# Output projection of a hybrid attention encoder: 256-column matmuls made 512 columns wide

## Chip, cores and metric

The kernel runs on one core of a Trainium2 chip. The metric is the device time of one execution in microseconds (us), as a median over runs.

## What is computed

Two layers act on x, 512 tokens by 1024 features. A layer normalises x, projects it to queries, keys, values and gates of two head groups (A: 8 heads of neighbourhood attention on an 8 by 64 grid; B: 4 heads of differential attention), multiplies each group's output by SiLU of its gate, and sends the concatenation y (512 by 1024; features 0 to 511 are group A, 512 to 1023 group B) through one output projection that is added to x. A last RMS norm closes the trunk.

```python
    h = rmsnorm(x, norm_g[l])
    proj = h @ w_in[l]
    ...
    y = jnp.concatenate([out_a * jax.nn.silu(g_a), out_b * jax.nn.silu(g_b)], axis=-1)
    x = x + y @ w_out[l]
return rmsnorm(x, final_g)
```

All is float32. The kernel keeps the precision by splitting each operand of a projection into a high part of type fp32r and a low part (the difference); a product is three matmuls: high times high, high times low, low times high.

## The kernel before

Tokens stand in four tiles of 128 (t = 0 to 3), features in eight chunks of 128 (kc). A weight unit is 1024 rows by 256 columns. `load_raw` (L79) reads one half of its rows (4 chunks, 512 KB) from DRAM on SP's queue into the tile `wraw` (two buffers). `load_unit` (L89) makes the high part `wh` by a ScalarE cast (L99) and the low part `wl` by a subtraction (L101), on GpSimd, or on VectorE for the first half of the units 16 to 19 of each 20, which are the output projection's; `wh` and `wl` have two buffers each. `Weights` hands the units out in the order of `seq` (L404 on): each `get` is followed by a `prefetch`, which emits the load and the conversion of the next unit.

Projections come in two forms. `proj_fm` (L245, matmul at L252) has the weights stationary and streams 512 tokens: 24 matmuls of 512 columns. `proj_tm` (L257, matmul at L267) has 128 tokens stationary and streams 256 weight columns: 24 matmuls of 256 columns (8 chunks times 3 terms) into half of a PSUM bank.

PSUM has eight banks: three in the pool `ps_p` (projections, tile `pp`), one in `ps_v` (attention output, `pv`), two each in `ps_s` (scores) and `ps_t` (transposes).

The output stage stands at the end of a layer. The gated outputs y are split into `yTh` and `yTl` (L569 on). Then four column units (`un`), and in each four token tiles: `proj_tm` over the chunks in the order 4, 5, 6, 7, 0, 1, 2, 3 (group B's features are ready first); VectorE adds the residual from PSUM (L592), ScalarE squares with a row sum into `sst` (L593), VectorE multiplies by the norm's weight (L595). In the last unit the row sums are added (L598), `rstd` makes the factor on GpSimd (L210, L212), and the normalised row is scaled. In layer 0 that is `norm_apply` (L226): two scalings on VectorE, eight transposes on TensorE (L234), and the split into `hTh` and `hTl` on ScalarE (L205) and VectorE (L206), which the next layer's projections read. In the last layer ScalarE (L601) and VectorE (L602) scale 384 and 640 columns, and the result is written to DRAM (L604).

The order of the instructions on each engine is not the order of the program text: a planner that simulates a timeline (`schedule_with_timeline_sim`) chooses it ahead of time, and on the chip each engine then keeps its order. So matmuls of the last attention heads stand among the first of the output stage, and the transposes and the next value projection among its last.

Of the kernel before, what the change touches and what calls it, by code (L numbers as in the profile page):

```python
# [9 lines left out]
F32 = mybir.dt.float32  # L10
F32R = mybir.dt.float32r
AF = mybir.ActivationFunctionType
ALU = mybir.AluOpType
# [3 lines left out]
P = 128  # L17
S = 512
D = 1024
# [4 lines left out]
NB = 4  # L24
# [20 lines left out]
def hybrid_encoder(ctx: ExitStack, tc: tile.TileContext, x, norm_g, w_in, na_rpb,  # L45
                   lambda_q1, lambda_k1, lambda_q2, lambda_k2,
                   subln_g, t5_table, w_out, final_g, na_mask, t5_onehot, out):
    nc = tc.nc
# [8 lines left out]
    small = ctx.enter_context(tc.tile_pool(name="small", bufs=6))  # L57
    dram = ctx.enter_context(tc.tile_pool(name="dram", bufs=1, space=DRAM))
    ps_p = ctx.enter_context(tc.tile_pool(name="ps_p", bufs=3, space=PSUM))
# [15 lines left out]

    # ---------------------------------------------------------------- weights
    unit_no = [0]

    def load_raw(parts, hf):  # L79
        r = wp.tile([P, 4, 256], F32, name="wraw", bufs=WRAW_BUFS)  # L80
        c = 0
        for src in parts:
            n_c = src.shape[1]
            nc.sync.dma_start(out=r[:, :, c:c + n_c],
                              in_=src.rearrange("(k p) c -> p k c", p=P)[:, 4 * hf:4 * hf + 4, :])
            c += n_c
        return r
# [35 lines left out]

    # ------------------------------------------------------- position biases
    tb_d = dram.tile([4, 1024], F32, name="tb_d")
# [58 lines left out]

    # ------------------------------------------------------------- lambdas
    def lambdas(l):
# [20 lines left out]

    # ---------------------------------------------------------------- norm
    def rstd(ss):
        G.tensor_scalar(out=ss, in0=ss, scalar1=1.0 / D, scalar2=1e-6, op0=ALU.mult, op1=ALU.add)  # L210
        rs = small.tile([P, 1], F32, name="rs")
        G.tensor_tensor(out=rs, in0=ss, in1=nhalf[:, 0:1], op=ALU.pow)  # L212
        return rs
# [29 lines left out]

    # --------------------------------------------------------- projections
    def proj_fm(w, col, c0=64):  # L245
# [55 lines left out]

    # ---------------------------------------------------------- attention B
    def attn_b(h, q, k, vt, yb, nlam, sg, yout):
# [57 lines left out]

    # ---------------------------------------------------------- attention A
    def attn_a(l, hd, half, q, k, vt, s_out):
# [37 lines left out]

    # ------------------------------------------------------------- schedule
    o_b = 2048
    seq = []  # L404
    for l in range(DEPTH):
        wi, wo = w_in[l], w_out[l]
        def qkc(o, i):
            return ((o + i * P, P), (o + 512 + i * P, P))

        def vgc(c):  # L410
            return ((c, 256),)

        unit = {"VB": lambda i: vgc(o_b + 1024 + 256 * i), "VA": lambda i: vgc(1024 + 256 * i),
                "QB": lambda i: qkc(o_b, i), "QA": lambda i: qkc(0, i),
                "GB": lambda i: vgc(o_b + 1536 + 256 * i), "GA": lambda i: vgc(1536 + 256 * i)}
        cols = [unit[u[:2]](int(u[2])) for u in ORDER if u[:2] in unit]
        seq += [[wi[:, c:c + n] for c, n in u] for u in cols]
        seq += [[wo[:, c:c + 256]] for c in (0, 256, 512, 768)]
    W = Weights(seq)
# [89 lines left out]
    for l in range(DEPTH):  # L509
# [73 lines left out]
        xn = [x2[:, i, :] for x2 in [big.tile([P, 2, D], F32, name="xn", tag="v") for _ in range(2)] for i in range(2)]  # L583
        sst = small.tile([P, NB, 4], F32, name="sst", bufs=1)
        yh, yl = ([y[:, i, :] for y in yt for i in range(2)] for yt in (yTh, yTl))
        for un in range(4):
            w = W.get()
            W.prefetch()
            for t in range(NB):
                pp = proj_tm(w, t * P, yh, yl, (4, 5, 6, 7, 0, 1, 2, 3))  # L590
                cs = slice(un * 256, (un + 1) * 256)
                V.tensor_tensor(out=xt[t][:, cs], in0=pp[:, 0:256], in1=xt[t][:, cs], op=ALU.add)  # L592
                A.activation(out=xn[t][:, cs], in_=xt[t][:, cs], func=AF.Square,  # L593
                             accum_out=sst[:, t, un:un + 1])
                V.tensor_tensor(out=xn[t][:, cs], in0=xt[t][:, cs], in1=g_bc[:, cs], op=ALU.mult)  # L595
                if un == 3:
                    ss = small.tile([P, 1], F32, name="ss")
                    V.tensor_reduce(out=ss, in_=sst[:, t, :], axis=mybir.AxisListType.X, op=ALU.add)  # L598
                    rs = rstd(ss)
                    if last:  # L600
                        A.activation(out=xn[t][:, 0:384], in_=xn[t][:, 0:384], func=AF.Copy, scale=rs)  # L601
                        V.tensor_scalar_mul(xn[t][:, 384:D], xn[t][:, 384:D], rs)  # L602
                        for i in range(2):
                            nc.sync.dma_start(out=out_v[2 * t + i], in_=xn[t][64 * i:64 * i + 64])  # L604
                    else:
                        nc.sync.dma_start(out=xs_d[t], in_=xt[t])
                        norm_apply(t, xt[t], None, xn[t], rs)

# [53 lines left out]
```

## Time and profile before

| | us |
|---|---|
| median of 3 runs | 633.57 |
| lowest, highest run | 631.53, 634.60 |
| span of the profiled execution | 630.6 |
| TensorE matmuls busy | 591.7 |
| VectorE busy | 422.3 |
| ScalarE busy | 324.6 |
| GpSimd busy | 277.3 |

The profile is one execution, with the time from its first to its last instruction as span. Engines are called PE (TensorE matmuls), PEld (its weight loads), DVE (VectorE), ACT (ScalarE), POOL (GpSimd) and SP. A line such as L267 is a line of the kernel. An instruction is written as engine, line, operation, output<-input tiles, size. In square brackets stands how long the engine was idle before it and what ended that. Matmuls overlap one another: the printed time of one is from its start to its modelled end, longer than the distance to the next.

### The profile page before, as it was taken

Reading aid. Unit: us, or ns where it says so; the run is one execution under the profiler, and the core shown is the slowest. Engines: PE = TensorE matmul, PEld = TensorE weight load, DVE = VectorE, ACT = ScalarE, POOL = GpSimd, SP = SyncE. Lnnn points to the kernel's source line nnn. Section 1 sums busy time; section 2 is a strip of 40 time slices with the busy share of each in tenths; the row PEclk is TensorE's granted clock in tenths of the full one; section 3 lists DMA queues with packets and bytes.
Section 4 is the critical chain, followed back from the end, with each engine's and each line's share of the span. In section 5 each row is a group of like instructions: output and inputs, shape, how many; then the busy total and the mean of one; then the engine's idle time right before and its main releaser. Section 6 shows DMA issues by size and latency. Waiting matters only on the chain.

```text
span 630.6 us, 10037 instructions
## 1 busy us (share of the span) xinstructions
PE 591.7 (94%) x3626; PEld 522.3 (83%) x3626; DVE 422.3 (67%) x907; ACT 324.6 (51%) x706; POOL 277.3 (44%) x232
## 2 busy tenths in 40 slices
PE   4799699999899999999999999999989999999992
PEld 3678597888799878889999898888879878889992
DVE  3552354997988868874564257798888968874542
ACT  3343353864766555744343455666567646654421
POOL 2341422444456747743143633344535665733111
PEclk9799899999999999999999999999999999999997
DMA  6566746552442454264454452342343444355204
GB/s 145 129 124 192 213 147 197 134 136 78 109 119 55 143 129 133 85 171 146 134 168 135 123 144 86 90 114 63 88 107 93 116 116 116 101 167 168 68 1 134
DMA packets 77448, 77.57 MB, mean 123 GB/s; under 512 B 9906, under 2 KB 71346, under 8 KB 76374
## 3 DMA queue, kind: packets, MB, share of 16 engines
q1 hardware_dynamic: 75926, 74.53, 41.7%
q0 software_dynamic: 1472, 2.40, 2.3%
q8 instruction: 29, 0.48, 0.3%
q14 instruction: 21, 0.17, 0.1%
HBM read 63.16 MB, written 9.37 MB: 115 GB/s over the span
## 4 chain that ended last, share of the span: by engine, by line
PE 58%; DMA 14%; DVE 10%; issue 5%; POOL 5%; SPq 5%; ACT 3%; POOLq 0%; ACTq 0%; DVEq 0%
PE pp L252 25%; PE pp L267 22%; DMA wraw<-in_w_in_dram 4%; DMA y<-in_x_dram 4%; SPq L135 3%; DVE ea L382 2%; POOL wl L101 2%; DMA yb_d<-tb_d 2%; POOL ba L179 2%; PE pv L338 2%; DVE kt L291 2%; DVE w4k L329 1%; PE pt L333 1%; PE st L316 1%; DMA rs_d<-rsb 1%
## 5 line engine op out<-in xcount | busy, mean ns | idle before, releaser
L101 POOL TENSOR_TENSOR wl<-wraw,wh 128x1024 fp32r<-128x1024 f32 x68 | 166.2, 2462 | 192.5 <-ACT wh L99 124.9
L99 ACT CAST wh<-wraw 128x1024 fp32r<-128x1024 f32 x78 | 78.8, 1046 | 72.2 <-DMA wraw<-in_w_in_dram 28.9
L252 PE MATMUL pp<-hTh,wh 128*128 128x512 f32 x384 | 103.4, 397 | 3.2 <-DVE kt L291 3.2
L252 PE MATMUL pp<-hTh,wl 128*128 128x512 f32 x384 | 106.3, 398 | 0.0
L252 PE MATMUL pp<-hTl,wh 128*128 128x512 f32 x384 | 104.5, 398 | 0.0
L252 PEld LDWEIGHTS pp<-hTh,wh 128*128 128x128 f32 x384 | 70.4, 188 | 17.7 <-issue 3.6
L252 PEld LDWEIGHTS pp<-hTh,wl 128*128 128x128 f32 x384 | 70.3, 189 | 14.5 <-issue 0.5
L252 PEld LDWEIGHTS pp<-hTl,wh 128*128 128x128 f32 x384 | 70.2, 188 | 13.9
L267 PE MATMUL pp<-wh,hTh 128*128 128x256 f32 x256 | 72.3, 302 | 7.7 <-ACT hTh L205 4.5
L267 PE MATMUL pp<-wh,yTh 128*128 128x256 f32 x256 | 72.4, 283 | 0.0
L267 PE MATMUL pp<-wl,yTh 128*128 128x256 f32 x256 | 72.3, 283 | 0.0
L267 PE MATMUL pp<-wh,yTl 128*128 128x256 f32 x256 | 71.9, 283 | 0.0
L267 PE MATMUL pp<-wh,hTl 128*128 128x256 f32 x256 | 70.3, 293 | 0.0
L206 DVE TENSOR_TENSOR ptl<-pt,pth 128x256 fp32r<-128x256 f32 (+1 forms) x96 | 48.2, 507 | 31.6 <-ACT pth L205 30.7
L267 PE MATMUL pp<-wl,hTh 128*128 128x256 f32 x256 | 68.9, 287 | 0.0
L205 ACT CAST pth<-pt 128x256 fp32r<-128x256 f32 (+1 forms) x96 | 42.0, 443 | 43.1 <-PE pt L333 29.3
L382 DVE TENSOR_SCALAR ea<-ea,rza 128x256 f32<-128x256 f32 x64 | 58.5, 914 | 1.8
L267 PEld LDWEIGHTS pp<-wh,hTh 128*128 128x128 f32 x256 | 49.3, 202 | 10.9 <-ACT hTh L205 5.0
L179 POOL TENSOR_TENSOR ba<-nmask,ya 128x256 f32<-128x256 f32 (+1 forms) x64 | 39.6, 650 | 32.3 <-DVE mna L376 18.5
L319 DVE CUSTOM_DVE_ANT_0 lt<-st,yb 128x512 f32<-128x512 f32 x64 | 43.5, 685 | 11.2 <-PE st L317 10.7
L267 PEld LDWEIGHTS pp<-wh,hTl 128*128 128x128 f32 x256 | 48.8, 199 | 0.8
L267 PEld LDWEIGHTS pp<-wh,yTh 128*128 128x128 f32 x256 | 49.1, 192 | 0.2
(111 smaller groups left out, 1141.0 us busy)
## 6 DMA issues: line engine op xcount, KB each, us to landing
wraw<-in_w_in_dram SPq DMA_DIRECT2D x32, 512.0 KB
wraw<-in_w_in_dram SPq DMA_DIRECT2D x64, 256.0 KB
kt<-kt SPq DMA_DIRECT2D x16, 512.0 KB
wraw<-in_w_out_dram SPq DMA_DIRECT2D x16, 512.0 KB
y<-in_x_dram SPq DMA_DIRECT2D x16, 256.0 KB
ya_d<-rp_d SPq DMA_DIRECT2D x32, 120.0 KB
ya<-ya_d SPq DMA_DIRECT2D x16, 240.0 KB
yb<-yb_d SPq DMA_DIRECT2D x8, 280.0 KB
```

Of the source, the lines that this page charges most:

```text
L99: A.copy(out=wh[:, ks, :], in_=r)
L101: eng.tensor_tensor(out=wl[:, ks, :], in0=r, in1=wh[:, ks, :].bitcast(F32), op=ALU.subtract)
L135: eng.dma_start(out=dst[:, i * C8:(i + 1) * C8, :], in_=bass.AP(tensor=src.tensor, offset=src.offset + base - step * r - C8 * b, ap=[[pitc ...
L179: G.tensor_tensor(out=ba[:, i0:i0 + n], in0=_view(nmask, i0 * C8, [[C8, n], [0, ROWS], [1, C8]]), in1=_view(y, w0, [[C8, n], [RPW, ROWS], ...
L205: A.copy(out=oh, in_=ps)
L206: V.tensor_tensor(out=ol, in0=ps, in1=oh.bitcast(F32), op=ALU.subtract)
L252: T.matmul(out=pp, lhsT=a[:, kc, cs], rhs=b[:, kc, c0:c0 + S], start=(n == 0), stop=(n == 3 * KC - 1))
L267: T.matmul(out=pp[:, 0:256], lhsT=a[kc][:, c0:c0 + P], rhs=b[:, kc, :], start=(n == 0), stop=(n == 3 * KC - 1))
L291: V.tensor_tensor(out=kl, in0=src, in1=kh.bitcast(F32), op=ALU.subtract)
L319: V.tensor_tensor_reduce(out=lt, in0=st, in1=yb[:, 48 - 16 * qt:560 - 16 * qt], scale=1.0, scalar=3e38, op0=ALU.add, op1=ALU.min, accum_ou ...
L338: T.matmul(out=pv[:, qp * 256:(qp + 1) * 256], lhsT=vt[:, kt, h % 2, vs, :], rhs=pp[:, kt, :], start=(n == 0), stop=(n == 11))
L382: V.tensor_scalar_mul(e, e, rz)
```

## The change

The output projection's weights are taken in pieces of 512 rows by 512 columns, in place of units of 1024 rows by 256 columns: for each column half first the rows of group B, then those of group A. A piece has as many bytes as a unit and lies in the same tiles, seen through `half_k` as four chunks of 512 columns; its two raw loads are one DMA each, of two chunks. For each of the two column halves, four PSUM banks (three `pp` and the one `pv`) hold the four token tiles while both pieces pass: 12 matmuls of 512 columns for each tile and piece. After the second piece a tile is evacuated with 512-column operations, and `sst` has two columns for each tile.

```diff
+    def half_k(z):
+        return z.rearrange("p (k a) c -> p k (a c)", a=2)
     def load_raw(parts, hf):
         r = wp.tile([P, 4, 256], F32, name="wraw", bufs=WRAW_BUFS)
+        if parts[0].shape[1] == S:
+            nc.sync.dma_start(out=half_k(r), in_=parts[0].rearrange("(k p) c -> p k c", p=P)[:, 2 * hf:2 * hf + 2, :])
+            return r
...
-        seq += [[wo[:, c:c + 256]] for c in (0, 256, 512, 768)]
+        seq += [[wo[r:r + S, c:c + S]] for c in (0, S) for r in (S, 0)]
...
-        for un in range(4):
-            w = W.get()
-            W.prefetch()
-            for t in range(NB):
-                pp = proj_tm(w, t * P, yh, yl, (4, 5, 6, 7, 0, 1, 2, 3))
-                cs = slice(un * 256, (un + 1) * 256)
-                V.tensor_tensor(out=xt[t][:, cs], in0=pp[:, 0:256], in1=xt[t][:, cs], op=ALU.add)
...
-                if un == 3:
...
+        def out_tile(un, t, cs, pp):
+            V.tensor_tensor(out=xt[t][:, cs], in0=pp, in1=xt[t][:, cs], op=ALU.add)
+            A.activation(out=xn[t][:, cs], in_=xt[t][:, cs], func=AF.Square,
+                         accum_out=sst[:, t, un:un + 1])
+            V.tensor_tensor(out=xn[t][:, cs], in0=xt[t][:, cs], in1=g_bc[:, cs], op=ALU.mult)
+            if un == 1:
...
+        for un in range(2):
+            pps = [ps_p.tile([P, S], F32, name="pp") for _ in range(3)] + [ps_v.tile([P, S], F32, name="pv")]
+            cs = slice(un * S, (un + 1) * S)
+            for half, c0 in enumerate((4, 0)):
+                wh, wl = (half_k(z) for z in W.get())
+                W.prefetch()
+                for t in range(NB):
+                    for kc in range(4):
+                        for i, (a, b) in enumerate(((yh, wh), (yh, wl), (yl, wh))):
+                            T.matmul(out=pps[t], lhsT=a[c0 + kc][:, t * P:(t + 1) * P], rhs=b[:, kc, :],
+                                     start=(half + kc + i == 0), stop=(half == 1 and kc == 3 and i == 2))
+                    if half == 1:
+                        out_tile(un, t, cs, pps[t])
```

What `out_tile` does for `un == 1` is what the loop did for `un == 3`.

## Rows read from the trace of the kernel before

**Rows 1.** The page: busy time of the engines; the chain that ended last, by engine.

```profile
PE 591.7 (94%) x3626; PEld 522.3 (83%) x3626; DVE 422.3 (67%) x907; ACT 324.6 (51%) x706; POOL 277.3 (44%) x232
...
PE 58%; DMA 14%; DVE 10%; issue 5%; POOL 5%; SPq 5%; ACT 3%; POOLq 0%; ACTq 0%; DVEq 0%
```

**Rows 2.** The chain in order of time, layer 1's stage: start us, us, what.

```profile
572.66 0.48 PE pp L267 x4
...
573.98 45.49 PE pp L267 x379
```

**Rows 3.** The same chain, end of layer 0's attention and its output stage.

```profile
270.23 7.43 PE pp L252 x32
...
278.12 3.97 PE pp L252 x17
...
283.40 44.42 PE pp L267 x369
```

**Rows 4.** Busy time by stretch, instructions in brackets, granted clock: ten us of layer 1's stage.

```profile
590.00:600.00 10.00, 10.00 (x86) 10.00 (x85) 4.88 (x9) 3.94 (x10) 1.37 (x1) 1.00 0.18 61
```

**Rows 5.** Timeline of ACT, POOL and DVE around a weight conversion: start us, us, instruction.

```profile
584.94 1.99 ACT L99 CAST wh<-wraw 128x1024 fp32r<-128x1024 f32 x2 [1.91 <-PE pp L267]
...
587.07 2.44 POOL L101 TENSOR_TENSOR wl<-wraw,wh 128x1024 fp32r<-128x1024 f32 x1 [8.94 <-ACT wh L99]
...
587.38 2.41 DVE L595 TENSOR_TENSOR xn<-y,g_bc 128x256 f32<-128x256 f32 x1
```

**Rows 6.** Timeline of VectorE: last read of the attention's bank in layer 1.

```profile
575.53 0.69 DVE L399 SCALAR_TENSOR_TENSOR y<-pv,tmpa 64x512 f32<-64x512 f32 x1
```

**Rows 7.** Tiles yTh, yTl, hTl: 512-column operations, ns min/median/max, first and last start.

```profile
L205 ACT CAST yTh<-y x16: 608/619/624, 265.3 to 578.2; 128x512 fp32r<-128x512 f32 x16
...
L206 DVE TENSOR_TENSOR yTl<-y,yTh x16: 679/692/2893, 266.2 to 578.8; 128x512 fp32r<-128x512 f32 x16
...
L206 DVE TENSOR_TENSOR hTl<-pt,hTh x16: 675/692/692, 15.6 to 341.7; 128x512 fp32r<-128x512 f32 x16
```

**Rows 8.** Timeline of VectorE, then ScalarE: last column unit of layer 1.

```profile
610.86 0.42 DVE L592 TENSOR_TENSOR y<-pp,y 128x256 f32<-128x256 f32 x1 [1.45 <-PE pp L267]
...
613.32 0.55 DVE L602 TENSOR_SCALAR xn<-xn,rs 128x640 f32<-128x640 f32 x1 [0.97 <-POOL rs L212]
...
613.79 0.42 DVE L592 TENSOR_TENSOR y<-pp,y 128x256 f32<-128x256 f32 x1
...
619.50 0.42 DVE L592 TENSOR_TENSOR y<-pp,y 128x256 f32<-128x256 f32 x1 [1.30 <-PE pp L267]
...
619.84 0.55 DVE L602 TENSOR_SCALAR xn<-xn,rs 128x640 f32<-128x640 f32 x1
...
620.50 0.42 DVE L595 TENSOR_TENSOR xn<-y,g_bc 128x256 f32<-128x256 f32 x1
...
621.93 0.55 DVE L602 TENSOR_SCALAR xn<-xn,rs 128x640 f32<-128x640 f32 x1 [0.94 <-POOL rs L212]
...
619.14 0.61 ACT L601 ACTIVATE xn<-xn,rs 128x384 f32<-128x384 f32 x1 [1.47 <-POOL rs L212]
...
619.95 0.42 ACT L593 ACTIVATE xn<-y 128x256 f32<-128x256 f32 x1 [0.20 <-DVE y L592]
```

**Rows 9.** Timeline of DVE, POOL, ACT and PE at the layer boundary.

```profile
331.26 0.42 DVE L592 TENSOR_TENSOR y<-pp,y 128x256 f32<-128x256 f32 x1
...
333.70 0.14 DVE L598 TENSOR_REDUCE ss<-sst 128x1 f32<-128x4 f32 x1
...
331.10 4.93 POOL L101 TENSOR_TENSOR wl<-wraw,wh 128x1024 fp32r<-128x1024 f32 x2 [1.27 <-ACT wh L99]
...
336.12 0.19 POOL L210 TENSOR_SCALAR ss<-ss 128x1 f32<-128x1 f32 x1
...
339.48 0.59 ACT L205 CAST hTh<-pt 128x512 fp32r<-128x512 f32 x1 [1.72 <-PE pt L234]
...
341.15 1.09 PE L252 MATMUL pp<-hTh,wh 128*128 128x512 f32 x4
```

More of the change, by code (lines that the diff above doesn't have):

```diff
@@ L583, in hybrid_encoder @@
         xn = [x2[:, i, :] for x2 in [big.tile([P, 2, D], F32, name="xn", tag="v") for _ in range(2)] for i in range(2)]
-        sst = small.tile([P, NB, 4], F32, name="sst", bufs=1)
+        sst = small.tile([P, NB, 2], F32, name="sst", bufs=1)
         yh, yl = ([y[:, i, :] for y in yt for i in range(2)] for yt in (yTh, yTl))
-        for un in range(4):
-            w = W.get()
-            W.prefetch()
-            for t in range(NB):
-                pp = proj_tm(w, t * P, yh, yl, (4, 5, 6, 7, 0, 1, 2, 3))
-                cs = slice(un * 256, (un + 1) * 256)
-                V.tensor_tensor(out=xt[t][:, cs], in0=pp[:, 0:256], in1=xt[t][:, cs], op=ALU.add)
-                A.activation(out=xn[t][:, cs], in_=xt[t][:, cs], func=AF.Square,
-                             accum_out=sst[:, t, un:un + 1])
-                V.tensor_tensor(out=xn[t][:, cs], in0=xt[t][:, cs], in1=g_bc[:, cs], op=ALU.mult)
-                if un == 3:
[L597 to L607, printed above, removed]
@@ new lines, in out_tile @@
+        def out_tile(un, t, cs, pp):
[4 more added lines that the diff above has]
+            if un == 1:
+                ss = small.tile([P, 1], F32, name="ss")
+                V.tensor_reduce(out=ss, in_=sst[:, t, :], axis=mybir.AxisListType.X, op=ALU.add)
+                rs = rstd(ss)
+                if last:
+                    A.activation(out=xn[t][:, 0:384], in_=xn[t][:, 0:384], func=AF.Copy, scale=rs)
+                    V.tensor_scalar_mul(xn[t][:, 384:D], xn[t][:, 384:D], rs)
+                    for i in range(2):
+                        nc.sync.dma_start(out=out_v[2 * t + i], in_=xn[t][64 * i:64 * i + 64])
+                else:
+                    nc.sync.dma_start(out=xs_d[t], in_=xt[t])
+                    norm_apply(t, xt[t], None, xn[t], rs)
```

## Prediction

> **What bounds the kernel.** I read the page first. TensorE is busy 94% of the span and has 58% of the chain that ended last; VectorE, the next engine, is busy 67% [rows 1]. The reader should note that the profiled execution spans 630.6 us while the median of the three timed runs is 633.57 us: some 3 us lie around the span, and I add every difference to the median. The chain in order of time then says what the stage under change waits for: in layer 1 it is one unbroken piece of 379 matmuls of line 267, 45.49 us, from 573.98 us to 619.47 us, and only then a tail of vector work [rows 2]; in layer 0 it is the same, 369 matmuls in 44.42 us [rows 3], and it begins and ends on TensorE there too. The table of stretches agrees: in 10 us of the stage TensorE and its weight loads are busy 10.00 us each at full clock, VectorE 4.88 us [rows 4]. So in this stage a nanosecond saved per matmul comes off the end, and work of the other engines costs nothing until TensorE waits for it. It could at two places: after the last matmul of layer 1, where nothing is left to hide it, and at the boundary.
>
> **TensorE's part.** The stage has 2 layers x 4 column units x 4 token tiles x 24 = 768 matmuls of 256 columns; after the change 2 x 2 x 2 x 4 x 12 = 384 of 512 columns. Products and columns streamed are the same; only what a matmul costs beyond its columns can go. The pitch, not the printed duration, is the price, as matmuls overlap: 45.49 us / 379 = 120.0 ns for 256 columns [rows 2]. For 512 columns the trace has the feature-major projections of line 252, same type, same 128x128 weight load: 32 in 7.43 us, 232.2 ns each, and 17 in 3.97 us, 233.5 ns [rows 3]. Before: 768 x 120.0 = 92.2 us. After: 384 x 232.2 = 89.2 us. The gain is 3.0 us. The other ends: by 233.5 ns it is 2.5 us. At the granted full clock (2.4 GHz) the columns alone take 106.7 and 213.3 ns, so the surplus is 13.3 ns at 256 and 18.9 ns at 512; were it a constant 13.3 ns per matmul, the pitch would be 226.6 ns and the gain 5.1 us. I take 3.0 us because thirty-two matmuls in a row are its row; 2.5 and 5.1 are kept for the range.
>
> The Trainium skill, "TensorE: Matmul & The Clock Gate", section "Wait — 56ns, not 53.3ns?", speaks for the constant: it gives a warm matmul its columns plus a fixed 2.5 ns or so whatever their number. By its own figures the gain would be an estimated 384 x 2.5 = 1.0 us; by its form with this trace's surplus at 256 columns it would be the 5.1 us. That form is the first rival. The trace agrees with neither so far, since its surplus grows with the columns, but its 512-column rows have another operand in the moving place.
>
> **Weights.** Each of the 16 raw loads of the output weights stays 512 KB, two per piece, on SP's queue at the same place; they only carry 512-column rows. The casts and subtractions keep their number, size and engine. A piece lasts 48 x 0.232 = 11.1 us instead of a unit's 96 x 0.120 = 11.5 us. In layer 1 a unit's weights are cast from 584.94 us, as soon as the buffer is free, and the last subtraction ends at 589.51 us, while they are needed a unit later, at about 596.4 us [rows 5]. That cover of 7 us becomes 6.5. I cost all of this at nothing; without the cover it would be up to 4.6 us a piece.
>
> **Banks.** Three projection banks and the attention's one are now held for two pieces (22.3 us), where a bank was held for one tile. The last reader before that, of the attention's bank, is the last neighbourhood head, which ends at 576.22 us [rows 6]; the last gate is read ahead of it. The first tile may start at 572.66 us [rows 2]; the third, which needs the last gate's bank, then starts 5.6 us later (578.2), the fourth, in the attention's bank, 8.4 us later (581.0). Covers: 2.0 us or more, and 4.8 us. For the second column half a bank's matmuls end three tiles (8.4 us) before it is needed, and its addition has that long. The next projection of layer 1 takes banks in the same turn as before, and the attention's bank is wanted only by the first attention head. Cost: nothing. That group A's features are wanted 11 us later is worth nothing either: TensorE has no stall there to win.
>
> **Evacuation and the tail.** There are 8 evacuations of 512 columns per layer in place of 16 of 256. VectorE's and ScalarE's total falls a little, which is worth nothing as both are half idle here. But what follows the last matmul gets longer: addition, square and multiplication each on 512 columns. VectorE takes 0.42 us on 256 columns for the addition and the multiplication [rows 8], and 0.69 us on 512, both from PSUM and from SBUF; ScalarE 0.42 us [rows 8] against 0.62 us [rows 7]. So +0.27 +0.20 +0.27 = +0.74 us on the tail that now runs from 619.50 us over the norm's factor to 621.93 us [rows 8]. One more delay can come: ScalarE's scaling of the third tile (619.14 us, 0.61 us) left ScalarE free 0.2 us before the last square [rows 8]. It comes 0.74 us later in its tile's chain, the last addition ends 0.27 us later in its own, and tiles follow each other after 12 x 0.232 = 2.79 us in place of 24 x 0.120 = 2.88: the last square is held up by some 0.3 us. The tail costs 0.74 to 1.05 us; I take 0.9, its middle. Below 0.74 it can hardly be, since the three steps follow one another. The transfers of the result (same number and size) follow as before.
>
> **The boundary.** The normalised tiles of layer 0 are transposed for layer 1 on TensorE. The last tile's chain in the trace: the addition starts at 331.26 us, behind other vector work, the reduction is done at 333.84, but GpSimd does its part at 336.12 only, since it subtracts weights from 331.10 to 336.03 [rows 9]. The longer steps (0.74 us) and some more lateness of the addition use up the 2.3 us for which the reduction's result lay there; GpSimd's subtraction is released by the end of the same matmuls as before. What is late next: the projections over all tokens start at 341.15 us with the first half of that tile's features, ready at 340.07 [rows 9], a cover of 1.1 us. I take nothing here; the other end stands under the second rival.
>
> **Sum.** -3.0 + 0.9 = -2.1 us: the span goes from 630.6 to 628.5, the median from 633.57 to 631.5 us, 0.33% less. A measurement of this kernel can tell about 0.5% (3.2 us) from no change, so this counts as the same. With the tail's ends and the pitch at 232.2 or 233.5 ns it is 631.3 to 632.1; the pitch's other end is the first rival.
>
> **Rivals.** First, the constant surplus: a matmul of 512 columns with the weights moving takes 226.6 ns. For it: the surplus has no reason in these rows to depend on the columns. Against it: every long run of line 252. Gain 5.1 - 0.9 = 4.2 us, 629.4 us, faster.
>
> Second, the vector chain, which ends slower. VectorE works in its own order, and in layer 1 the first tile's last scaling stood ahead of the second's addition [rows 8]: it came 2.46 us after its own addition (610.86 to 613.32), and the next addition 0.47 us after that (613.79). With 0.74 us more, a tile's turn is 2.46 + 0.74 + 0.47 = 3.67 us, against 2.79 us on TensorE, so the fourth tile is 3 x 0.88 = 2.6 us late. At the boundary the same 2.6 + 0.74 us stands against 1.1 us of cover: 2.2 us. Together -3.0 + 0.74 + 2.6 + 2.2 = +2.5 us, 636.1 us. If besides one 512-wide multiplication is caught by GpSimd's weight subtraction, as one of 256 columns was (2.41 us in place of 0.42) [rows 5], 1.7 us more, 637.8 us. It decides where the additions of the next tile stand behind the scaling; against it speaks that the last addition, ready first, did stand ahead of the scaling (619.50 before 619.84) [rows 8], and an order by readiness would now put every addition ahead.
>
> Third, no gain per matmul: with weights as the moving operand 512 columns take twice the 120.0 ns. Then only the tail remains: 634.5 us, the same. Against it: in the 256-column rows the moving weights show nothing special. Fourth, the order elsewhere: it is made by a simulated timeline, and the layer after the change may be ordered differently, two us either way (629.5 or 633.5 with the rest as forecast). Against it: the stage's long pieces begin 290.58 us apart in the two layers and hold 369 and 379 matmuls, so the order repeats [rows 2, 3].
>
> **Chances.** Forecast 0.58, constant surplus 0.13, vector chain 0.17, no gain 0.06, order elsewhere 0.06. Faster by over 0.5% (under 630.4): the constant surplus, half of the order, and 0.03 of the forecast, as the runs themselves scatter (631.53 to 634.60), 0.19. Slower by over 0.5% (over 636.7): two thirds of the vector chain, that with the caught multiplication or with more of it, 0.11. The rest, 0.70, is within 0.5%. The range reaches from 629.0, just under the constant surplus, to 636.2, the vector chain without the caught multiplication.
>
> **What would show it.** Line 252's pitch on the new matmuls: 384 of them, four pieces of about 11.1 us a layer, TensorE busy 10.00 of 10 us in both stages; a pitch near 226 ns speaks for the first rival, 240 for the third. The tail from the last addition to the last scaling: 2.43 us before, about 3.2 to 3.5 after. At the boundary no TensorE wait; a wait of TensorE for the split of a transposed tile, or a last addition of layer 1 more than 1 us behind the last matmul, speaks for the second rival. Wrong throughout would be: a wait of TensorE for a bank or for weights between pieces.

## The result, and the profile after

| | before | after |
|---|---|---|
| median | 633.57 us | 637.18 us |
| lowest, highest run | 630.08, 636.05 | 633.23, 641.73 |
| runs | 13 | 13 |
| span of the profiled execution | 630.6 us | 640.0 us |

The ratio is 1.0070, 95% interval 1.0046 to 1.0094: slower by 2.9 to 6.0 us, where 2.1 us less was forecast. The two spans differ by more, 9.3 us, since the profiled execution of after is its slowest (641.73 us) and 3.65 us of its span were lost ahead of the first matmul of the changed stage, in work that is the same in both kernels. So what follows compares distances inside the spans: from the first matmul of layer 0's output stage to that of layer 1's (the period), the stage itself, and the tail behind the last matmul's start.

The chain that ended last, in order of time (start us, us, what), first from layer 0's stage to the next layer's projections, then the start of layer 1's stage:

```profile
287.60 7.28 PE pp L619 x32
...
308.25 8.16 PE pp L619 x36
...
323.37 2.29 DVE xn L596
...
331.11 0.56 POOL rs L218
331.69 5.04 DVE xn L232 x2
336.74 0.61 DVE hTl L212
...
337.39 1.11 PE pt L240 x4
338.50 2.56 PE pp L273 x12
...
584.99 7.28 PE pp L619 x32
```

The new matmuls (L619) follow each other after 8.16 us / 36 = 226.7 ns, and 7.28 us / 32 = 227.5 ns. Both stages last 44.05 us from the first to the last start, against 46.68 us in layer 1 before: 2.63 us less, and 5.3 us for two layers. TensorE is busy 10.00 us in both stretches of 10 us below, and has no wait in either stage. The gain is there, then, and larger than forecast.

It is given back between the layers: there the chain runs over VectorE, with 5.04 us in two scalings (L232), before TensorE can go on at 337.39. The period, which the long pieces give as 573.98 - 283.40 = 290.58 us before [rows 2, 3], is 584.99 - 287.60 = 297.39 us after: 6.8 us longer, though it holds one shortened stage. The boundary costs 6.8 + 2.6 = 9.4 us more than before.

Busy time by stretch, with the granted clock as the eighth number (after the five engines' times): layer 0's stage, layer 1's stage, and the boundary of after:

```profile
290.00:300.00 10.00, 10.00 (x46) 8.29 (x45) 2.07 (x3) 2.63 (x3) 2.22 (x3) 1.00 0.62 202
595.00:605.00 10.00, 10.00 (x45) 8.28 (x45) 5.69 (x7) 4.18 (x8) 2.43 (x1) 1.00 0.36 105
...
330.00:334.00 4.00, 1.40 (x11) 0.95 (x9) 3.65 (x5) 3.57 (x6) 3.08 (x4) 0.89 0.65 266
334.00:338.00 4.00, 0.61 (x3) 0.61 (x4) 4.00 (x6) 0.00 (x0) 2.45 (x1) 0.50 0.48 141
338.00:342.00 4.00, 4.00 (x21) 4.00 (x20) 1.29 (x2) 0.63 (x2) 0.74 (x2) 0.50 0.40 121
```

TensorE has 0.61 us of work in the four us from 334; the granted clock is at its lower level (0.50, that is 1.2 of 2.4 GHz) in all of 334 to 342, also after the work is back: 21 instructions in 338 to 342, where the kernel with the change in layer 1 only (e1 below) has 37 at full clock:

```profile
338.00:342.00 4.00, 4.00 (x37) 4.00 (x35) 2.43 (x5) 1.32 (x3) 0.00 (x0) 1.00 0.44 131
```

The waits of TensorE from 318 to 350 us (total, times, longest), and the timelines of TensorE, VectorE, ScalarE and GpSimd that explain them:

```profile
PE pt L240 <- DVE hTl L212: 4.3, 1, 4.3
PE pp L273 <- ACT hTh L211: 1.7, 1, 1.7
```

```profile
329.86 1.03 PE L240 MATMUL pt<-ident,xn 128*128 128x128 f32 x8
332.63 0.39 PE L273 MATMUL pp<-wh,hTh 128*128 128x256 f32 x1 [1.74 <-ACT hTh L211]
...
326.70 0.88 DVE L232 TENSOR_SCALAR xn<-xn,rs 128x512 f32<-128x512 f32 x2 [0.37 <-POOL rs L218]
...
331.69 5.04 DVE L232 TENSOR_SCALAR xn<-xn,rs 128x512 f32<-128x512 f32 x2 [0.35 <-POOL rs L218]
336.66 0.68 DVE L212 TENSOR_TENSOR hTl<-pt,hTh 128x512 fp32r<-128x512 f32 x1
...
330.10 1.99 ACT L105 CAST wh<-wraw 128x1024 fp32r<-128x1024 f32 x2 [0.50 <-issue]
332.00 0.58 ACT L211 CAST hTh<-pt 128x512 fp32r<-128x512 f32 x1
...
331.11 0.55 POOL L218 TENSOR_TENSOR rs<-ss,nhalf 128x1 f32<-128x1 f32 x1
331.62 4.83 POOL L107 TENSOR_TENSOR wl<-wraw,wh 128x1024 fp32r<-128x1024 f32 x2
```

Three things come together. (a) The first tile's eight transposes (L240) now stand behind the stage's last matmul (329.62); before they stood ten matmuls ahead of its end (L234 below). So nothing of TensorE's own is left to cover what follows. (b) The cast of the transposed half (L211, 332.00) stands on ScalarE behind two weight casts (330.10): 1.7 us. (c) The third tile's two scalings on VectorE (L232) take 5.04 us in place of 0.88, for as long as GpSimd's two weight subtractions run (331.62 to 336.45); the split of the first tile's second half (L212) is queued behind them: 4.3 us. With 1.7 + 4.3 = 6.0 us of waiting and about 6 us of work at half clock (337.4 to 343.4, an estimated 3 us lost) the 9.4 us are explained but for 0.4.

Before, the weight subtraction stood in nearly the same place (331.10, 4.93 us [rows 9]), but no scaling fell into it. From the timelines of TensorE, GpSimd and VectorE before:

```profile
327.66 1.03 PE L234 MATMUL pt<-ident,xn 128*128 128x128 f32 x8
...
329.61 0.28 PE L267 MATMUL pp<-wh,yTl 128*128 128x256 f32 x1
...
329.29 0.55 POOL L212 TENSOR_TENSOR rs<-ss,nhalf 128x1 f32<-128x1 f32 x1
...
329.87 0.88 DVE L226 TENSOR_SCALAR xn<-xn,rs 128x512 f32<-128x512 f32 x2 [0.26 <-POOL rs L212]
...
336.97 0.49 DVE L226 TENSOR_SCALAR xn<-xn,rs 128x512 f32<-128x512 f32 x1 [1.33 <-POOL rs L212]
```

GpSimd's order is the same in both kernels: the third tile's factor, the two subtractions, the last tile's factor. What differs is the time of the third tile's factor. Before, it was done at 329.84 and the subtractions then still waited, 1.27 us in all, for ScalarE's cast [rows 9]; in that gap the scalings (329.87) ran undisturbed, and the last tile's (336.97) came behind the subtractions. In after the factor is done at 331.66, the cast is there, and the subtractions start at once; the scalings, which that same factor releases, start 0.07 us behind them. The factor is 1.8 us later at the same end of the stage (329.61 and 329.62). The three longer steps are 0.74 us of that. Another part comes from the first tile, whose multiplication (L596, 323.37 in the chain above) was itself caught by the unit before's subtractions, 2.29 us in place of 0.69; VectorE's later additions come behind it.

The end, VectorE and ScalarE's last tile; compare [rows 8]:

```profile
627.44 0.69 DVE L593 TENSOR_TENSOR y<-pv,y 128x512 f32<-128x512 f32 x1
628.42 0.55 DVE L603 TENSOR_SCALAR xn<-xn,rs 128x640 f32<-128x640 f32 x1 [0.29 <-POOL rs L218]
628.92 0.69 DVE L596 TENSOR_TENSOR xn<-y,g_bc 128x512 f32<-128x512 f32 x1
...
628.17 0.63 ACT L594 ACTIVATE xn<-y 128x512 f32<-128x512 f32 x1 [1.48 <-DVE y L593]
...
630.62 0.62 ACT L602 ACTIVATE xn<-xn,rs 128x384 f32<-128x384 f32 x1 [1.23 <-POOL rs L218]
```

From the last addition to the end of the last scaling it is 3.80 us, before 3.05 (619.50 to 622.55): +0.75. The whole tail, from the start of the last matmul to the end, is 12.94 us against 11.44: +1.5. How much of that is the change's is taken up below.

### The profile page after: what moved, and what is told of

It is laid out like the page before. It is cut to its first block, busy times and chain, and to the rows that moved or that the text cites. A ratio compares the mean times of both kernels' runs of the same rounds, so it can differ in the third digit from the quotient of the medians.

```text
span 640.0 us, 9199 instructions
## 1 busy us (share of the span) xinstructions
PE 593.1 (93%) x3242; PEld 507.9 (79%) x3242; DVE 416.6 (65%) x875; ACT 320.3 (50%) x674; POOL 276.3 (43%) x232
## 4 chain that ended last, share of the span: by engine, by line
PE 60%; DMA 13%; DVE 11%; issue 5%; POOL 4%; SPq 4%; ACT 2%; POOLq 0%; ACTq 0%; DVEq 0%
PE pp L258 26%; PE pp L273 11%; PE pp L619 9%; DMA y<-in_x_dram 4%; DMA wraw<-in_w_in_dram 3%; SPq L141 3%; PE pv L344 3%; DVE ea L388 3%; PE pv L619 3%; DMA yb_d<-tb_d 2%; PE st L322 2%; PE pt L339 2%; PE st L323 2%; POOL wl L107 2%; PE st L376 1%
## 5 line engine op out<-in xcount | busy, mean ns | idle before, releaser
L273 PE MATMUL pp<-wh,hTl 128*128 128x256 f32 x256 | 71.7, 299 | 0.0
L212 DVE TENSOR_TENSOR ptl<-pt,pth 128x256 fp32r<-128x256 f32 (+1 forms) x96 | 48.2, 507 | 35.0 <-ACT pth L211 34.2
L273 PE MATMUL pp<-wl,hTh 128*128 128x256 f32 x256 | 70.5, 294 | 0.0
L211 ACT CAST pth<-pt 128x256 fp32r<-128x256 f32 (+1 forms) x96 | 42.0, 442 | 45.1 <-PE pt L339 31.2
L273 PEld LDWEIGHTS pp<-wl,hTh 128*128 128x128 f32 x256 | 49.3, 201 | 0.7
L328 ACT ACTIVATE w4k<-lt,mn 128x512 f32<-128x512 f32 x64 | 46.0, 722 | 4.3 <-DVE mn L325 3.9
L385 ACT ACTIVATE ea<-ea,mna 128x256 f32<-128x256 f32 x64 | 32.8, 512 | 23.0 <-DVE mna L382 23.0
L297 DVE TENSOR_TENSOR kt<-pp,kt 64x512 fp32r<-64x512 f32 x32 | 21.9, 685 | 27.7 <-ACT kt L296 27.3
```

What stands on the lines that cost most here:

```text
L211: A.copy(out=oh, in_=ps)
L212: V.tensor_tensor(out=ol, in0=ps, in1=oh.bitcast(F32), op=ALU.subtract)
L273: T.matmul(out=pp[:, 0:256], lhsT=a[kc][:, c0:c0 + P], rhs=b[:, kc, :], start=(n == 0), stop=(n == 3 * KC - 1))
L328: A.activation(out=e[:, m, :].rearrange("p (b r c) -> p b r c", r=ROWS, c=C8), in_=lt.rearrange("p (r b c) -> p b r c", r=ROWS, c=C8), fun ...
L385: A.activation(out=e, in_=e, func=AF.Exp, bias=mn, scale=-1.0, accum_out=z[:, j:j + 1])
```

## Experiments

Each ratio is against runs of the kernel before on the same chip. Period, waits, clock (the lowest of the stretches of 4 us from 326 to 350) and tail are from each kernel's one profile; line numbers shift by a few where lines were added. A difference of the medians and one by the ratio can lie up to 1.0 us apart (after: 3.6 and 4.4 us), so the text says which is meant.

| | period us | waits of TensorE at the boundary us | lowest clock | tail us | median us (before) | ratio, 95% interval |
|---|---|---|---|---|---|---|
| before | 290.6 | none | 1.00 | 11.44 | 633.57 | |
| after | 297.4 | 4.3 + 1.7 | 0.50 | 12.94 | 637.18 (633.57) | 1.0070 (1.0046 to 1.0094) |
| e1 | 292.3 | none | 1.00 | 12.76 | 633.23 (636.0) | 0.9966 (0.9942 to 0.9991) |
| e2 | 297.6 | 4.3 + 1.7 | 0.51 | 12.21 | 640.42 (636.0) | 1.0079 (1.0052 to 1.0106) |
| e3 | 293.6 | 2.3 + 0.2 | 0.62 | 12.70 | 634.38 (636.0) | 0.9983 (0.9962 to 1.0003) |
| e4 | 294.8 | 2.4 + 1.7 | 0.50 | 12.91 | 637.06 (636.0) | 1.0032 (1.0005 to 1.0058) |
| e5 | 296.4 | 5.0 + 0.2 | 0.50 | 12.89 | 638.65 (635.45) | 1.0051 (1.0027 to 1.0075) |
| e6 | 290.1 | 0.7 | 1.00 | 12.92 | 632.67 (635.45) | 0.9950 (0.9926 to 0.9975) |
| e7 | 292.3 | 2.3 | 0.74 | 12.18 | 635.11 (635.45) | 0.9998 (0.9977 to 1.0018) |
| e9 | 289.1 | 0.2 | 1.00 | 12.47 | 632.01 (634.5) | 0.9947 (0.9922 to 0.9972) |
| e10 | 288.7 | 0.2 | 1.00 | 12.16 | 631.85 (634.5) | 0.9948 (0.9923 to 0.9973) |
| e11 | 290.5 | 1.0 + 0.4 | 1.00 | 12.73 | 633.98 (634.5) | 0.9987 (0.9968 to 1.0005) |

**e1 and e2: the change in one layer.** The loop, the weight pieces and `sst` of one layer as after, of the other as before (`sst` under a name for each layer); e1's is shown, e2 has `l == 0` in its place.

```diff
-        seq += [[wo[r:r + S, c:c + S]] for c in (0, S) for r in (S, 0)]
+        if l == 1:
+            seq += [[wo[r:r + S, c:c + S]] for c in (0, S) for r in (S, 0)]
+        else:
+            seq += [[wo[:, c:c + 256]] for c in (0, 256, 512, 768)]
...
```

> The change in layer 1 alone; layer 0 keeps the four 256-column units. In the trace after, layer 1's stage took 44.12 us from its first matmul to its last (46.81 before) and the tail behind it 12.75 us (11.13 before). If the loss sits at the layer boundary alone, this kernel gains 2.7 and loses 1.6 us: about 632.5 us against 633.6 of before. If the loss is spread over both stages, or sits in the tail, it comes out above 634 us.

> The change in layer 0 alone, with the old tail. If the boundary carries the loss: -2.7 us of matmuls and some 7.4 us at the boundary (the measured +3.6 us, less -5.4 of both stages' matmuls and +1.6 of the tail), about 638.3 us. If the boundary's waits of the one trace are an accident of that execution: about 631 us.

Layer 1 alone gains 2.2 us by the ratio: the stage is 2.63 us shorter and the tail 1.3 us longer, and its boundary shows no wait. Its period is 1.7 us longer than before's all the same, 1.3 us of it one wait of TensorE in layer 0's stage (for ScalarE's split of y), which the profile of before does not have; so a difference of 1 or 2 us between two periods says little by itself. Layer 0 alone loses 5.0 us by the ratio, with the waits of after to the tenth and the same overlap of VectorE and GpSimd:

```profile
326.85 5.05 DVE L232 TENSOR_SCALAR xn<-xn,rs 128x512 f32<-128x512 f32 x2 [0.35 <-POOL rs L218]
...
326.78 4.83 POOL L107 TENSOR_TENSOR wl<-wraw,wh 128x1024 fp32r<-128x1024 f32 x2
```

So the loss is the boundary's; pitch, weights, banks and tail together are a gain.

**e3: the boundary's scalings on ScalarE.**

```diff
-                V.tensor_scalar_mul(xn[:, cs], xn[:, cs], rs)
+                A.activation(out=xn[:, cs], in_=xn[:, cs], func=AF.Copy, scale=rs)
```

> The changed kernel with the two scalings per tile at the layer boundary on ScalarE in place of VectorE. Theory of the caught scaling: one scaling of the third tile took 5.04 us in place of 0.88 on VectorE while GpSimd subtracted weights, the split and the transposes queued behind it. On ScalarE it is not caught, TensorE does not wait, its clock stays at full: -5.4 + 1.6 us, about 629.8 us. Theory of the long chain: the longer 512-column steps make the tiles late by themselves; then TensorE still waits some 4 us and the time stays at 635 or more.

Of the two waits the long one shrinks from 4.3 to 0.2 us. The other grows from 1.7 to 2.3 us, since ScalarE now has the scalings to do as well, and the clock still falls (0.62). The median is 1.6 us below before's where 3.8 us were expected, and the interval still reaches no change:

```profile
PE pp L273 <- ACT hTh L211: 2.3, 1, 2.3
PE pt L240 <- DVE hTl L212: 0.2, 1, 0.2
```

While GpSimd subtracts here (331.95, 5.15 us), VectorE's splits of transposed tiles, which read PSUM, take 0.69 us as ever, while a multiplication with both operands in SBUF takes 0.98 us in place of 0.69. What is caught is VectorE's work from SBUF to SBUF.

**e4: the subtractions of that weight unit on VectorE.** Nothing of GpSimd is left there to collide with; TensorE's order is that of after.

```diff
-            eng = V if n == 2 or (n % 20 >= 16 and hf == 0) else G
+            eng = V if n in (2, 21) or (n % 20 >= 16 and hf == 0) else G
```

> The changed kernel with the two weight subtractions that ran on GpSimd from 331.62 us on VectorE in place of it (two times 1.23 us). The order of TensorE is the same. Theory of the caught scaling: the scaling falls from 5.04 to 0.88 us, but the two subtractions stand in front of the split, so that TensorE's wait falls from 6.0 to about 2 to 2.6 us and the clock may fall for a shorter time: about 632 to 633 us. Theory of the long chain: VectorE has more to do, TensorE waits longer, 638 us or more.

```profile
328.99 0.88 DVE L232 TENSOR_SCALAR xn<-xn,rs 128x512 f32<-128x512 f32 x2 [0.35 <-POOL rs L218]
329.79 2.35 DVE L107 TENSOR_TENSOR wl<-wraw,wh 128x1024 fp32r<-128x1024 f32 x2
332.06 0.68 DVE L212 TENSOR_TENSOR hTl<-pt,hTh 128x512 fp32r<-128x512 f32 x1
```

The scalings are back at 0.88 us, but VectorE now does the subtraction itself, 2.35 us ahead of the split: the wait shrinks from 4.3 to 2.4 us, and the time stays above before's. That wait had been expected, 2 to 2.6 us in all. What the expectation left out is the other one, 1.7 us behind ScalarE's casts, which this edit does not touch: together they are 4.1 us, and the clock falls to 0.50 again.

**e5: that unit's conversion held back.** `held` keeps what is emitted since a mark behind a given instruction of the same engine: here the casts behind the first tile's split, the subtractions behind the last tile's factor.

```diff
-                W.prefetch()
+                if last or un == 0 or half == 0:
+                    W.prefetch()
...
+                        if un == 1 and not last:
+                            for tt, eng in ((0, nc.scalar), (3, nc.gpsimd)):
+                                if t == tt:
+                                    hold[eng.engine] = [i for i in nc.cur_bb.bb.instructions if i.engine == eng.engine][-1].name
+                            if t == 3:
+                                mark = len(nc.cur_bb.bb.instructions)
+                                W.prefetch()
+                                held(mark, hold)
```

> The changed kernel with one weight conversion (the unit whose buffer the last piece of layer 0 frees) kept behind the boundary's norm work: its casts stand behind the first tile's split on ScalarE, its subtractions behind the last tile's factor on GpSimd. No engine gets other work, and TensorE's order is the same. If the two waits of TensorE at the boundary come from this conversion (1.7 us: the split behind the casts; 4.3 us: the scaling caught by the subtractions), the second goes, the clock stays at full, and of the first the way from the transposes over the cast remains, about 1 us: 2 to 3 us below the kernel before. If they come from the longer vector steps, TensorE still waits 4 us or more, and the time lies above that of the kernel before.

A miss, and the most telling one: the subtraction was moved from the third tile's scalings straight into the fourth's. It follows the factor that releases them at once, as in after, and starts 0.07 us ahead of them.

```profile
335.61 5.08 DVE L232 TENSOR_SCALAR xn<-xn,rs 128x512 f32<-128x512 f32 x2 [0.35 <-POOL rs L218]
...
335.54 4.87 POOL L107 TENSOR_TENSOR wl<-wraw,wh 128x1024 fp32r<-128x1024 f32 x2
```

The first wait (ScalarE's casts) fell from 1.7 to 0.2 us, where about 1 us was expected to remain; the second is there again, 3.7 us behind the caught scalings, with 1.2 us more in which the first tile's split waited behind the third tile's scaling and TensorE, its transposes done last, had nothing else.

**e6: e5 with the first tile's transposes ahead of the last six matmuls of the stage.**

```diff
+                            if un == 1 and half == 1 and not last and t == 3 and kc == 2:
+                                mark = len(nc.cur_bb.bb.instructions)
...
+                            if un == 1 and half == 1 and not last and t == 3 and kc == 2 and i == 0:
+                                held(mark, {nc.tensor.engine: tr0[0]})
...
+                        if un == 1 and not last and t == 0:
+                            tr0 = [[i for i in nc.cur_bb.bb.instructions if i.engine == nc.tensor.engine][-1].name]
```

> As the run before, and the first tile's eight transposes stand ahead of the last six matmuls of layer 0's stage in place of behind them, as they stood in the kernel before. If the rest of the first wait is the way from the transposes to the split, it goes: 3.5 to 4 us below the kernel before (5.4 us of matmuls less 1.5 us of tail). If the first tile's scaling is too late for that, TensorE waits ahead of the transposes instead, and nothing is gained against the run before.

2.8 us below before by the medians, 3.2 by the ratio, short of the 3.5 to 4 us expected. The catch is still there, one scaling in each subtraction as in e5, but now a split stands between the two scalings, and by then TensorE has the next projection's matmuls at hand: 0.7 us of waiting in all, and the granted clock stays at 1.00.

```profile
335.87 2.56 DVE L232 TENSOR_SCALAR xn<-xn,rs 128x512 f32<-128x512 f32 x1
338.35 0.68 DVE L212 TENSOR_TENSOR hTl<-pt,hTh 128x512 fp32r<-128x512 f32 x1
338.95 2.00 DVE L232 TENSOR_SCALAR xn<-xn,rs 128x512 f32<-128x512 f32 x1
...
335.74 4.92 POOL L107 TENSOR_TENSOR wl<-wraw,wh 128x1024 fp32r<-128x1024 f32 x2
```

**e7: e6 with the square written to the PSUM bank just read,** so that the multiplication need not wait for it.

```diff
-            A.activation(out=xn[t][:, cs], in_=xt[t][:, cs], func=AF.Square,
+            A.activation(out=pp, in_=xt[t][:, cs], func=AF.Square,
```

> As the run before, and the square's elements go to the PSUM bank that was just read, so that the multiplication by the norm's weight no longer waits for the square. One 512-column step (0.63 us) leaves the chain behind the last matmul: the tail is 0.6 us shorter, 4 to 4.6 us below the kernel before. If the tail is set by the results' transfers, nothing changes against the run before.

The tail fell by 0.74 us, to 12.18: 0.42 us of it between the last addition and the end of the last scaling (3.80 to 3.38 us), the rest behind that. The boundary gave back more: both of the last tile's scalings stood side by side again, with no split between them (334.65, 4.79 us beside GpSimd's 334.28, 4.88 us), and TensorE waited 2.3 us. It is the catch of e5, and nothing in the edit asked for that order.

**e9 and e10: e6 with the last tile's scalings on ScalarE; then also e7's square in the last layer only.**

```diff
-                V.tensor_scalar_mul(xn[:, cs], xn[:, cs], rs)
+                if t == NB - 1:
+                    A.activation(out=xn[:, cs], in_=xn[:, cs], func=AF.Copy, scale=rs)
+                else:
+                    V.tensor_scalar_mul(xn[:, cs], xn[:, cs], rs)
...
-            A.activation(out=xn[t][:, cs], in_=xt[t][:, cs], func=AF.Square,
+            A.activation(out=pp if last else xn[t][:, cs], in_=xt[t][:, cs], func=AF.Square,
```

> e6 (unit 21's conversion held, first tile's transposes ahead of the stage's last six matmuls) with the two scalings of the last tile, and of that tile alone, on ScalarE. In e6's profile these two stood on VectorE while GpSimd subtracted and took 2.56 and 2.00 us instead of 0.5; TensorE's waits behind them are short, 0.2 and 0.6 us. Theory (the overlap of VectorE's scaling and GpSimd's subtraction is a cost wherever it falls): no VectorE instruction over 1.3 us is left at the boundary and TensorE has no wait above 0.3 us there; 0.8 us less than e6, about 3.6 us below before (ratio 0.994). Rival (the overlap is covered once the matmuls of the next layer are there): the time of e6, ratio 0.995, or up to 1 us more, because ScalarE's two scalings (1.3 us) now stand ahead of its casts of hTh.

> e9, and in the last layer alone the square is written to the PSUM bank that the addition has just read, so that the multiplication by the final gain need not wait for the square to have written its tile. Theory (the tail is the chain addition, square, factor, scaling, and the square's place in it is what the multiplication waits for): the stretch from the last matmul to the end falls from 12.9 to 12.2 us, as in e7; 0.7 us less than e9. Rival (the tail is set by the output transfers behind it): no difference to e9.

e9's timeline has GpSimd's subtraction beside ScalarE's scalings, and neither is longer for it; what VectorE does meanwhile reads PSUM:

```profile
336.04 1.34 ACT L233 ACTIVATE xn<-xn,rs 128x512 f32<-128x512 f32 x2
...
335.49 4.76 POOL L107 TENSOR_TENSOR wl<-wraw,wh 128x1024 fp32r<-128x1024 f32 x2
```

The period is 289.1 us, 1.0 us less than e6 and 1.5 less than before. By the ratios e9 and e6 can't be told apart (0.9947 and 0.9950 on two chips), nor e10 from e9 (tails of 12.16 and 12.47 us; from the last addition to the end of the last scaling 3.38 and 3.80): what was expected of each step is below what the runs resolve. Both e9 and e10 are faster than before (2.5 and 2.65 us by the medians) and than after.

**e11: e3 with e6's early transposes, and nothing held.**

> The changed kernel with all boundary scalings on ScalarE (e3) and the first tile's eight transposes ahead of the stage's last six matmuls, and nothing held: with the transposes early, ScalarE's casts of the first tile stand ahead of unit 21's weight casts by themselves. Theory (two causes, each taken away: scalings caught by the subtraction, casts of the first tile behind weight casts): both of TensorE's long waits gone, the granted clock whole through the boundary; e3's 0.998 less the remaining 2.3 us wait and 1.7 us of half clock: ratio about 0.993, close to e9. Rival (ScalarE becomes the late engine, eight scalings of 0.67 us each among its casts): waits of 1 to 2 us behind hTh casts, ratio 0.996 to 0.998.

0.9987, nearer to the rival than to the theory. The casts of the first tile do stand ahead of the weight casts by themselves, and the clock stays at 1.00. But TensorE waits 0.4 us for a cast of ScalarE and 1.0 us, in two, for splits of VectorE; ahead of the second of these a multiplication is caught, SBUF to SBUF again, 2.06 us in place of 0.69:

```profile
335.26 2.06 DVE L596 TENSOR_TENSOR xn<-y,g_bc 128x512 f32<-128x512 f32 x1
...
332.02 4.74 POOL L107 TENSOR_TENSOR wl<-wraw,wh 128x1024 fp32r<-128x1024 f32 x2 [0.27 <-ACT wh L105]
```

**e8 and e12: why 227 ns here and 232 ns in the feature-major projections.** e8 exchanges the output projection's inner loops (products outside, chunks inside) as the feature-major projection has them; e12 is e10 with the opposite exchange there.

```diff
-                    for kc in range(4):
-                        for i, (a, b) in enumerate(((yh, wh), (yh, wl), (yl, wh))):
+                    for i, (a, b) in enumerate(((yh, wh), (yh, wl), (yl, wh))):
+                        for kc in range(4):
```

> The changed kernel with the loops over the four chunks and over the three products exchanged in the output projection, the order that the feature-major projections have. The new matmuls follow each other after 226.8 ns, those of the feature-major projections after 232.2 ns, at the same size. If the order of the products makes the difference, the pitch here rises to about 232 ns; if it is the operands (which one stays, which one moves), it stays at about 227 ns. The time is that of the changed kernel but for up to 2 us.

> e10 with the loops of the feature-major projection (the other 512-column matmuls, 232 ns each in every run so far) exchanged to the order of the output projection: chunks of the features outer, the three products inner. e8, the exchange the other way round, left the output projection at 227 ns. If the order of the products matters after all on this side, the pitch of the feature-major matmuls falls from 232 to about 227 ns, 5 us less over some 1,100 of them; if it hangs on what moves and what stands (here the tokens' features move and the weights stand, in the output projection the reverse), the pitch stays at 232 and the time is e10's, or 1 to 3 us more, since the low halves are now needed in the first chunk rather than after eight matmuls.

From the chains of e8 and of e12:

```profile
309.49 8.16 PE pp L619 x36
```

```profile
226.50 5.57 PE pp L261 x24
```

8.16 / 36 = 226.7 ns and 5.57 / 24 = 232.1 ns: the order of the products changes neither. (e8's one run took 643.05 us; its profile has after's boundary. e12 took 651.99 us, ratio 1.026, 1.018 to 1.034: among the waits that it adds is one for scores behind VectorE, 9.0 us in two.) What is left as a difference is which operand moves and which stands, or where the two lie; neither was tried by itself, so the cause of the 5 ns stays open.

## Why the prediction was wrong

**TensorE's part: right in kind, too small.** The term of 3.0 us measured 5.3 (2.63 us per layer, from layer 1). The step that failed here is the choice of line 252's row for the new pitch; the other end named there, a constant surplus, held: 226.7 - 213.3 = 13.4 ns at 512 columns against 13.3 at 256. The doubt "another operand in the moving place" was the right one. The rule of the Trainium skill that was weighed there ("TensorE: Matmul & The Clock Gate", section "Wait — 56ns, not 53.3ns?") agrees in form for the matmuls with the weights moving, a fixed surplus whatever the columns; its size, 2.5 ns, is not what these runs show, and line 252's matmuls keep 18.8 ns (e12).

**Weights and banks: right.** No wait of TensorE between the pieces in either layer, and 10.00 of 10 us busy.

**Tail: 0.9 us forecast, 1.5 in the two profiles, of which 0.85 can be laid to the change.** The three longer steps cost the 0.74 us that were worked out (0.75). The square was not held up as feared. Missing in the sum was the last matmul's own longer run (0.39 us against 0.28, so that the addition starts 0.1 us later). The remaining 0.6 us lie between the end of the last scaling and the end (631.24 to 639.95, against 622.55 to 630.62), and they are not shown to be the change's: e2, whose layer 1 is as before, has 8.84 us there and a tail of 12.21 us, and over all profiles that stretch is 8.07 (before) to 8.88 us.

**Boundary: this is the step that failed, and it decided the sign.** It was costed at nothing and cost 9.4 us in the profiles; with 5.3 us less on TensorE and 1.5 more in the tail that makes 5.6 us, inside the 2.9 to 6.0 measured. The cost had been taken from one chain, the last tile's. That chain was read rightly, and it was the wrong one. The step took the order around it as given, with the transposes among the stage's last matmuls as before, and looked for what would be late in that order. The planner moved them behind the last matmul, so the first tile's split became what TensorE waits for, and the third tile's factor came so late that its scalings fell into GpSimd's subtractions. The rows for it were there: a multiplication of 2.41 us beside a subtraction [rows 5], a subtraction of 4.93 us [rows 9], which in the trace of before lies between the third tile's scalings (329.87) and the fourth's (336.97). The question "which VectorE instructions from SBUF to SBUF fall into these 4.9 us, if tiles come 0.1 us closer and each chain is 0.74 us longer?" was put for the multiplications of a rival and not for the scalings.

**The rivals.** The constant surplus was true of the pitch and false of the time: 629.4 us wanted an undisturbed boundary. With the boundary mended e9 and e10 are 2.5 and 2.65 us below before; that rival's gain of 4.2 us lies inside their intervals (1.7 to 5.0 us), and 1.1 us (e9) and 0.8 us (e10) of a shortened stage's 2.6 don't arrive in the one period that each has. That rival is thus neither shown nor ruled out for a mended boundary. The vector chain's 636.1 to 637.8 us hold the measured median by luck, for its mechanism did not happen: the last addition of layer 1 starts at 627.44 us, as the last matmul ends, so no tile fell behind there, and no addition stood behind a scaling. One piece of it did happen, in layer 0: a 512-column multiplication caught by GpSimd's subtraction, 1.6 us longer where 1.7 was put. The large catch, of two scalings, it did not have. "Order elsewhere" was the nearest in kind; two us was too small for it, and the equal spacing of the two stages before says nothing about an order that is made anew.

**What would have shown it** named a TensorE wait for the split of a transposed tile at the boundary as the sign of a slower kernel; that wait, 4.3 us, is the row that is there.

Shown by the runs: the loss is the boundary's (e1, e2); the long wait follows the overlap of scaling and subtraction wherever this is put (e3, e5, e7, e9), and the transposes' place (e5 against e6) and a split between the two scalings (e6 against e7) go with how much of it TensorE feels. Several edits moved more than one thing in the order, so these two are not parted. Not settled: why the planner moved the transposes.

## What to carry to other kernels

A change that shortens a TensorE stage moves every instruction that the planner packs around its end, so cost the boundary with the order open: list what VectorE does from SBUF to SBUF near each long GpSimd instruction, and price each at the length of that instruction. Look first at what GpSimd does right behind the instruction whose result releases VectorE: in after, e2, e5, e6 and e7 the long instruction started there at once, and each time VectorE was caught; before, it started 1.3 us later, and VectorE was through. A wait of TensorE can cost twice, once as idle time and once as work at the lower clock after it: here 6.0 us of waiting and some 3 us more, while the 1.4 us of e11, in three pieces, left the clock at 1.00. And take a pitch from rows with the same operand moving, or keep the other end as the forecast's equal.

## What the runs showed of the hardware

GpSimd's subtraction (two of 2.4 us) holds up VectorE's fp32 scaling until it ends (0.88 us for two scalings becomes 5.04, 5.05, 5.08, 4.79) and a multiplication of two SBUF operands as well (0.69 becomes 2.06 to 2.29), while additions and splits that read PSUM (0.68 us) and ScalarE's scalings (1.34 us) run beside it unharmed. The Trainium skill, "SBUF — State Buffer", section "SBUF: two separate sides", has an exclusive lock of one port pair between these two engines, for the whole instruction; the trace agrees. Two subtractions in a row catch two scalings one by one. In after, with the second subtraction from 333.93 to 336.45:

```profile
331.69 2.56 DVE L232 TENSOR_SCALAR xn<-xn,rs 128x512 f32<-128x512 f32 x1 [0.35 <-POOL rs L218]
...
334.18 2.56 DVE L232 TENSOR_SCALAR xn<-xn,rs 128x512 f32<-128x512 f32 x1
```

Each scaling ends 0.3 us behind a subtraction (333.97 and 336.45). So the first gets through at the change from one subtraction to the next, and the second, started when that next one already runs, waits again; e5 has the same (2.60 and 2.56 us).

The work ahead of layer 0's stage, the same in all, took 280.7 to 287.5 us in thirteen profiles of before, after and the experiments without e12. In after, one stretch there had the granted clock at 0.52, where before had 1.00:

```profile
111.00:118.00 7.00, 5.97 (x20) 5.30 (x21) 5.87 (x13) 6.49 (x15) 6.38 (x6) 0.52 0.63 151
```

```profile
111.00:118.00 7.00, 7.00 (x39) 5.60 (x38) 6.81 (x17) 6.29 (x14) 4.81 (x6) 1.00 0.81 201
```

The first fence is of after, the second of before: 20 matmuls against 39 in the same 7 us. A difference of one pair of spans is therefore worth little by itself here; distances inside a span are worth more.
